# q and k of the first attention block: transposed by a trip through HBM and VectorE in place of TensorE

## The chip, the cores and the metric

The kernel runs on one core of one Trainium2 chip. The metric is device time in microseconds (us) of one execution of the whole layer, lower is better; the kernel before is given as the median of three runs. Engines are named as the profile names them: PE is TensorE (PEld its weight loads), DVE is VectorE, ACT is ScalarE, POOL is GpSimd and SP is SyncE, which here only issues transfers.

## The reference

One decoder layer on 256 tokens of width 2048, in float32. What the change touches is block A, a dilated sliding-window attention with 8 heads of 128; block B, a latent attention with 8 heads, the output projection and the MLP follow.

```python
h = _rmsnorm(x, norm_attn_pre)
proj = h @ w_in                        # columns: A.q | A.k | A.v | B.c_q | B.c_kv | B.k_rope
a_q = _rope(a_q.reshape(B, S, 8, 128), positions, 32)      # rotary on the first 32 of 128 channels
a_k = _rope(a_k.reshape(B, S, 8, 128), positions, 32)
...                                    # three windows: (128,1), (512,4), (2048,16), causal
s = einsum('...ihd,...jhd->...hij', q, k) * 128 ** -0.5    # per head: q times k transposed
p = exp(s - max(s)); o = (p / sum(p)) @ v                  # the three outputs merged by their sums
...
x = x + _rmsnorm(concat(A, B) @ w_out)
x = x + _rmsnorm(relu(rmsnorm(x) @ w_up) ** 2 @ w_down)
```

With 256 tokens the three windows fold into one softmax with a bias per query and key (a table that the host makes), so a head of block A is one score product, one softmax and one product with v.

## The kernel before

The tokens lie in two blocks of 128 (`b`), tokens on the partitions. Every big product is done in three passes over a value split in two (`hi` and `lo`: hi·hi, hi·lo, lo·hi), so each weight tile that comes from HBM into a `raw` buffer is rounded by ACT (`hi`, line 311) and subtracted by DVE (`lo`, line 312) before PE uses it. SP issues the weight loads (line 195). There are 5 `raw` buffers and 8 pairs of `hi` and `lo`, and a tile's split stands in the engines' queues 6 tiles ahead of the PE work that uses it.

The input projection of block A runs in two halves of four heads each: first `acc_qk` (q and k of heads 0 to 3 together), `acc_v`; then `acc_q`, `acc_k`, `acc_v` of heads 4 to 7; then the projections of block B (`acc_ckv`, `acc_cq`). ACT brings each result from PSUM to SBUF with the row's norm (`evac_a`, line 675), DVE applies the rotary table in four instructions (`rope`, lines 615 to 618).

The heads of a half (`heads_a`, line 651) are worked on while PE does the projections of what comes next. Per head: four PE transposes of a 128x128 piece of q or k into one PSUM bank (line 659, through the helper at line 305), one DVE copy of that bank to SBUF (`qkT_a`, line 661), the score product (`sc_a`, two matmuls, which show as four rows), the softmax on DVE and ACT, three more transposes (`pT_a`), and the product with v (`o_a`). Two chains of two heads each run at a distance of `D_PAIR`.

Each engine takes its instructions strictly in program order, and the program is written by a planner (`Flow`): every stretch of work is a generator that yields estimated waits, the planner keeps a clock that PE work moves on (0.109 us for a transpose, 0.216 us for a 512 column matmul), and between the matmuls of a projection it lets those generators write their next instructions whose due time has come. So a number in a `yield` decides between which matmuls an attention instruction stands on PE, and between which splits it stands on ACT and DVE.

In block A the host hands the tokens over in an order in which, inside a block of 128, token 32·(p mod 4) + p div 4 stands in row p. The MLP of the kernel uses this already: it writes 128x512 pieces of its middle result to HBM in another order (line 965), reads them back (line 978) and has DVE transpose the 32x32 blocks (line 980).

Of the kernel before, what the change touches and what calls it, by code (L numbers as in the profile page):

```python
# [26 lines left out]
P = 128  # L27
# [8 lines left out]
RA = 32  # L36
# [51 lines left out]
DA = (3.0, 0.5, 3.0, 3.0, 4.0, 3.0, 0.5)  # L88
DB = (2.5, 0.5, 2.0, 3.0, 3.0, 2.0)
D_PAIR, D_KR = 3.5, 10.0  # L90
D_X0, D_X, D_SS, D_TAB = 8.0, 3.0, 3.0, (14.0, 20.0)
D_NORM, D_HT, D_SECOND = 4.5, 1.5, 4.0

# [175 lines left out]
def layer(nc, tc, io):  # L269
# [23 lines left out]
    def tp_bank(name):  # L293
        return next_bank(4, 2, name)
# [214 lines left out]

    mix = pool("mix", "right")  # L510
    pa = pool("pa", "right")
    mixT = [mix.tile([P, HA + HB, S], F32R, name=f"mixT_{w}") for w in ("hi", "lo")]
    mix.tile([P, 64], F32, name="mix_pad")
    xT = [pa.tile([P, KD, S], F32R, name=f"xT_{w}") for w in ("hi", "lo")]
# [67 lines left out]
    def tables():  # L582

        yield D_TAB[0]
        nc.scalar.dma_start(out=pos_i, in_=io["pos"])
        nc.scalar.dma_start(out=cst, in_=io["consts"])
        yield D_TAB[1]
        pos_f = con.tile([P, NB], F32, name="pos_f")
        nc.vector.tensor_copy(pos_f, pos_i)
        ang = pa.tile([P, 2, NB, 96], F32, tag="qkT", bufs=2, name="ang")  # L590
        kk_ = pa.tile([P, 2, NB, 96], F32, tag="qkT", bufs=2, name="kk_")
        for w in range(2):
            for b in range(NB):
                nc.vector.tensor_scalar_mul(ang[:, w, b, :], freq[:, w * 96:(w + 1) * 96], pos_f[:, b:b + 1])
            nc.vector.tensor_scalar(kk_[:, w], ang[:, w], 1.0 / (2 * np.pi), 0.25 * w, op0=OP.mult, op1=OP.add)
        yield 1.0
        nc.vector.tensor_scalar(kk_, kk_, MAGIC, -MAGIC, op0=OP.add, op1=OP.add)
        for c in (C1, C2, C3):
            nc.vector.scalar_tensor_tensor(out=ang, in0=kk_, scalar=-c, in1=ang, op0=OP.mult, op1=OP.add)
        yield 1.0  # L600
        nc.vector.tensor_scalar_add(ang[:, 1], ang[:, 1], float(np.pi / 2))
        nc.vector.tensor_scalar(ang, ang, PI_LO, -PI_LO, op0=OP.min, op1=OP.max)
        yield 4.0
        nc.scalar.activation(trig, ang, AF.Sin)
# [43 lines left out]
        split(mixT[0][:, head, :], mixT[1][:, head, :], o[:, :S])  # L648


    def heads_a(qkv, half, hs, after):
        while any(c in flow.chains for c in after):
            yield 0.5
        for h in hs:
            nm = f"a{half}{h}"
            tp = tp_bank(f"qkT_{nm}")
            for i, w in enumerate("qk"):
                for b in range(NB):
                    transpose(tp[:, (2 * i + b) * P:(2 * i + b + 1) * P], qkv[w][:, b, h * 128:(h + 1) * 128])
            qkT = pa.tile([P, 512], F32, tag="qkT", bufs=2, name=f"qkT_{nm}")  # L660
            nc.vector.tensor_copy(qkT, tp)
            yield DA[0]
            sc = at_bank(f"sc_{nm}")
            mm(sc[:, 0:128], qkT[:, 0:128], qkT[:, 256:384], True, True, MM)
            mm(sc[:, 128:384], qkT[:, 128:256], qkT[:, 256:512], True, True, 2 * MM)
            yield DA[1]
            yield from softmax_pv(pa, DA, sc, bias_a, SCALE_A,
                                  [qkv["v"][:, b, h * 128:(h + 1) * 128] for b in range(NB)], half * 4 + h, nm)
            yield DA[6]

    def evac_a(t, accs, nm, half):
        while pre in flow.chains:
            yield 0.5
        for b in range(NB):
            nc.scalar.activation(t[:, b, :], accs[b][0], AF.Copy, scale=rstd0[0][:, b:b + 1])
        yield 1.0
        while tab in flow.chains:
            yield 0.5
        if nm != "v":
            tv = t.rearrange("p b (h d) -> p b h d", d=128)[:, :, :, :RA]  # L680
            rope(pa, tv, tv, RA // 2, 4, 0, f"{nm}{half}")

    pre = flow.start(prelude())
    tab = flow.start(tables())
# [1 line left out]
    for half in range(2):  # L686
        qkv = {}
        for nms in (("qk", "v") if not half else "qkv"):
            accs = [acc for _, _, acc in proj(xT, [ch_a[half, nms]], f"{nms}{half}",
                                              bank_of=at_bank if (half, nms) == (0, "v") else None)]  # L690
            for i, nm in enumerate(nms):
                t = pa.tile([P, NB, 512], F32, tag=nm, name=f"{nm}_{half}")
                qkv[nm] = t
                evacs.append(flow.start(evac_a(t, [[acc[i]] for acc in accs], nm, half)))
            flow.pump()
        flow.finish(*heads)
        heads = [flow.start(heads_a(qkv, half, hs, evacs), 2.0 + d) for hs, d in (((0, 1), 0.0), ((2, 3), D_PAIR))]


    lat = pool("lat", "left")  # L700
    ckv = lat.tile([P, NB, KVR + RB], F32, name="ckv")
    cq = lat.tile([P, NB, QR], F32, name="cq")
# [23 lines left out]
    for _, b, acc in proj(xT, [ch_ckv], "ckv"):  # L726
        for i in range(2):
            nc.scalar.activation(ckv[:, b, i * 288:(i + 1) * 288], acc[i][:, :288], AF.Copy, scale=rstd0[0][:, b:b + 1])
    kv_chain = flow.start(latent(ckv, 0, "kv", lat), 2.0)
    for _, b, acc in proj(xT, [ch_cq], "cq"):  # L730
        nc.scalar.activation(cq[:, b, :], acc[0], AF.Copy, scale=rstd0[0][:, b:b + 1])
    flow.finish(kv_chain, *heads)
# [658 lines left out]
```

## Time and profile before

| what | value |
|---|---|
| three runs | median 1036.33 us, 1035.93 to 1036.93 |
| the profiled execution | 1035.85 us |
| its span, first to last instruction | 1034.1 us |
| granted TensorE clock, mean | 0.997 |
| busy: PE, DVE, ACT, POOL | 1022.4, 834.4, 634.6, 63.5 us |
| instructions: PE, DVE, ACT, POOL | 4718, 1125, 850, 100 |
| moved by DMA | 253.44 MB, mean 245 GB/s |

The span is shorter than the profiled execution by 1.75 us, which lie outside the first and the last instruction. Matmuls are pipelined: the duration of one in the profile is longer than the time by which it puts off the next. The chain of waits gives the time that each piece of work held the end of the program back; that is the view in which PE work has a price.

### The profile page before, as it was taken

What the parts mean: (1) busy time and instruction counts of PE and PEld (TensorE: products, weight loads), DVE (VectorE), ACT (ScalarE), POOL (GpSimd) and SP (SyncE); (2) the same over time, 40 slices, a digit from 0 to 9 for tenths busy, and PEclk for the clock granted to TensorE, in tenths of its full rate; (3) what the DMA queues carried; (4) which work ended last, traced back from release to release, by engine and by line L of the source; (5) the groups of instructions that cost most, each with busy time, mean ns of one, the idle gap of its engine ahead of it and who ended that gap; (6) DMA issues with size and microseconds to landing.
All of it is one profiled execution on the core that took longest, in us unless ns stands there. A gap on an engine that the chain in (4) does not pass through costs nothing.

```text
span 1034.1 us, 13262 instructions
## 1 busy us (share of the span) xinstructions
PE 1022.4 (99%) x4718; PEld 851.3 (82%) x4718; DVE 834.4 (81%) x1125; ACT 634.6 (61%) x850; POOL 63.5 (6%) x100
## 2 busy tenths in 40 slices
PE   9999999999999999999999999999999999999996
PEld 6888889889888878888888888888888888888885
DVE  6675536577547669999999999898999999899795
ACT  6585536566446467666775767666666665767571
POOL 0000000000001010000100100000101000211100
PEclk9999999999999999999999999999999999999998
DMA  8975447554438478877989887589989867888962
GB/s 288 361 237 166 138 136 223 155 163 144 144 122 263 142 276 284 272 239 258 285 258 302 269 262 258 191 275 335 354 267 366 299 240 258 302 314 303 329 240 82
DMA packets 105298, 253.44 MB, mean 245 GB/s; under 512 B 8720, under 2 KB 29712, under 8 KB 104848
## 3 DMA queue, kind: packets, MB, share of 16 engines
q1 hardware_dynamic: 65744, 175.14, 50.8%
q0 software_dynamic: 16112, 57.68, 16.8%
q10 hardware_dynamic: 23376, 19.78, 6.1%
q8 instruction: 37, 0.61, 0.2%
q14 instruction: 29, 0.24, 0.1%
HBM read 224.78 MB, written 27.79 MB: 244 GB/s over the span
## 4 chain that ended last, share of the span: by engine, by line
PE 96%; DVE 1%; DMA 1%; issue 1%; ACT 0%; POOL 0%; DVEq 0%; POOLq 0%; SPq 0%; ACTq 0%
PE acc_u L301 26%; PE y L301 25%; PE acc_o L301 8%; PE md L301 6%; PE m L301 6%; PE acc_v L301 4%; PE acc_qk L301 4%; PE acc_ckv L301 2%; PE acc_ukv L301 2%; PE acc_q L301 2%; PE acc_cq L301 2%; PE acc_k L301 2%; PE acc_uq L301 2%; PE sc_b L301 1%; DMA raw<-in_w_in 1%
## 5 line engine op out<-in xcount | busy, mean ns | idle before, releaser
L312 DVE TENSOR_TENSOR lo<-raw,hi 128x1024 fp32r<-128x1024 f32 (+3 forms) x207 | 234.1, 1149 | 83.9 <-ACT hi L311 82.5
L311 ACT ACTIVATE hi<-raw 128x1024 fp32r<-128x1024 f32 (+3 forms) x207 | 203.4, 996 | 70.9 <-DMA raw<-in_w_in 16.8
L301 PE MATMUL acc_u<-hi,hT_lo 128*128 128x512 f32 x386 | 150.3, 389 | 0.4 <-DVE hT_lo L312 0.4
L301 PE MATMUL acc_u<-hi,hT_hi 128*128 128x512 f32 x386 | 150.7, 390 | 0.0
L301 PE MATMUL acc_u<-lo,hT_hi 128*128 128x512 f32 x386 | 150.2, 389 | 0.0
L301 PE MATMUL y<-hi,uhi 128*128 128x512 f32 x358 | 139.3, 389 | 0.0
L301 PE MATMUL y<-lo,uhi 128*128 128x512 f32 x358 | 139.3, 389 | 0.0
L301 PE MATMUL y<-hi,ulo 128*128 128x512 f32 x358 | 139.3, 389 | 0.0
L315 ACT ACTIVATE hi<-raw,gcol 128x1024 fp32r<-128x1024 f32 x86 | 97.0, 1148 | 33.1 <-PE acc_u L301 18.2
L316 DVE SCALAR_TENSOR_TENSOR lo<-raw,gcol,hi 128x1024 fp32r<-128x1024 f32 x86 | 106.7, 1273 | 9.4 <-ACT hi L315 9.3
L301 PEld LDWEIGHTS acc_u<-hi,hT_lo 128*128 128x128 f32 x386 | 72.5, 188 | 15.9 <-DVE hT_lo L312 0.8
L301 PEld LDWEIGHTS acc_u<-lo,hT_hi 128*128 128x128 f32 x386 | 72.5, 188 | 14.9
L301 PEld LDWEIGHTS acc_u<-hi,hT_hi 128*128 128x128 f32 x386 | 72.5, 188 | 14.7
L301 PEld LDWEIGHTS y<-hi,uhi 128*128 128x128 f32 x358 | 67.2, 188 | 14.1
L301 PEld LDWEIGHTS y<-lo,uhi 128*128 128x128 f32 x358 | 67.2, 188 | 13.9
L301 PEld LDWEIGHTS y<-hi,ulo 128*128 128x128 f32 x358 | 67.2, 188 | 13.9
L312 DVE TENSOR_TENSOR lo<-st_down,hi 128x1024 fp32r<-128x1024 f32 x46 | 55.0, 1219 | 0.6 <-ACT hi L311 0.6
L301 PE MATMUL acc_o<-hi,mixT_hi 128*128 128x512 f32 x128 | 51.8, 405 | 0.0
L311 ACT ACTIVATE hi<-u 128x1024 fp32r<-128x1024 f32 (+1 forms) x33 | 32.2, 979 | 29.7 <-PE acc_u L301 11.7
L301 PE MATMUL acc_o<-hi,mixT_lo 128*128 128x512 f32 x128 | 50.2, 392 | 0.0
L301 PE MATMUL acc_o<-lo,mixT_hi 128*128 128x512 f32 x128 | 50.0, 390 | 0.0
L311 ACT ACTIVATE hi<-st_down 128x1024 fp32r<-128x1024 f32 x46 | 47.8, 1049 | 3.5 <-DVE st_down L371 2.1
(338 smaller groups left out, 2018.9 us busy)
## 6 DMA issues: line engine op xcount, KB each, us to landing
raw<-in_w_up SPq DMA_DIRECT2D x86, 512.0 KB, 4.8
raw<-in_w_down SPq DMA_DIRECT2D x82, 512.0 KB, 6.1
raw<-in_w_in SPq DMA_DIRECT2D x55, 512.0 KB, 5.1
ab<-in_w_up POOLq DMA_DIRECT2D x17, 1024.0 KB, 7.4
raw<-in_w_out SPq DMA_DIRECT2D x32, 512.0 KB, 4.4
ab_down<-in_w_down POOLq DMA_DIRECT2D x11, 1024.0 KB, 8.9
ulo<-ukeep POOLq DMA_DIRECT2D x20, 512.0 KB, 6.4
rkeep<-r ACTq DMA_DIRECT2D x28, 256.0 KB, 3.4
```

The lines of the kernel that those rows point to most:

```text
L301: nc.tensor.matmul(out, a, b, start=start, stop=stop)
L311: nc.scalar.activation(hi, src, AF.Copy)
L312: nc.vector.tensor_tensor(out=lo, in0=src, in1=hi.bitcast(F32), op=OP.subtract)
L315: nc.scalar.activation(hi, src, AF.Copy, scale=g)
L316: nc.vector.scalar_tensor_tensor(out=lo, in0=src, scalar=g, in1=hi.bitcast(F32), op0=OP.mult, op1=OP.subtract)
```

## The change

The PE transposes of q and k and the DVE copy behind them are gone. Instead, after the rotary step, each of q and k of a half makes a trip: POOL issues two stores (one per token block, 256 KB each) to a scratch tensor in HBM in an order that puts every 32x32 block's channels next to each other, then two loads that bring it back, and DVE transposes the 32x32 blocks of the returned tile into the place from which the score product reads. To make room for the trip the tiles of q and k have three slots of 512 columns in place of two (ACT writes slots 1 and 2, DVE writes slots 0 and 1), and those of the first half lie in a pool of their own (`early`) that is given up before block B's latents are placed. ACT writes q and k in another column order (channels of the four heads interleaved in groups of 32), so its read from PSUM is strided.

New waits in the planner: 2.0, 5.0 and 13.0 (first half) or 9.0 (second) between rotary step, stores, loads and DVE transposes, and a delay of 2.5 before the heads start. The first half's heads so stand later in the program; before v of the second half is brought from PSUM they are now finished.

```diff
+D_LOADED, D_LATENT = (13.0, 9.0), 3.5
...
+    early = pool("early", "left")
...
-    def heads_a(qkv, half, hs, after):
+    def heads_a(qkv, half, hs, after, delay):
         while any(c in flow.chains for c in after):
             yield 0.5
+        yield delay
         for h in hs:
             nm = f"a{half}{h}"
-            tp = tp_bank(f"qkT_{nm}")
-            for i, w in enumerate("qk"):
-                for b in range(NB):
-                    transpose(tp[:, (2 * i + b) * P:(2 * i + b + 1) * P], qkv[w][:, b, h * 128:(h + 1) * 128])
-            qkT = pa.tile([P, 512], F32, tag="qkT", bufs=2, name=f"qkT_{nm}")
-            nc.vector.tensor_copy(qkT, tp)
-            yield DA[0]
+            qT, kT = [qkv[w][:, :2, h * P:(h + 1) * P] for w in "qk"]
             sc = at_bank(f"sc_{nm}")
-            mm(sc[:, 0:128], qkT[:, 0:128], qkT[:, 256:384], True, True, MM)
-            mm(sc[:, 128:384], qkT[:, 128:256], qkT[:, 256:512], True, True, 2 * MM)
+            mm(sc[:, 0:128], qT[:, 0], kT[:, 0], True, True, MM)
+            mm(sc[:, 128:384], qT[:, 1], kT, True, True, 2 * MM)
...
         for b in range(NB):
-            nc.scalar.activation(t[:, b, :], accs[b][0], AF.Copy, scale=rstd0[0][:, b:b + 1])
+            out, a = t[:, b + (nm != "v"), :], accs[b][0]
+            if nm != "v":
+                out, a = [v.rearrange(f"p ({o}) -> p a h c", a=4, h=4) for v, o in ((out, "a h c"), (a, "h a c"))]
+            nc.scalar.activation(out, a, AF.Copy, scale=rstd0[0][:, b:b + 1])
...
-        if nm != "v":
-            tv = t.rearrange("p b (h d) -> p b h d", d=128)[:, :, :, :RA]
-            rope(pa, tv, tv, RA // 2, 4, 0, f"{nm}{half}")
+        if nm == "v":
+            return
+        tv = t[:, 1:, :128].rearrange("p b (h d) -> p b h d", d=RA)
+        rope(pa, tv, tv, RA // 2, 4, 0, f"{nm}{half}")
+        keeps = [dram.tile([P, 512], F32, name=f"keep{nm}{half}{b}") for b in range(NB)]
+        yield 2.0
+        for b in range(NB):
+            nc.gpsimd.dma_start(out=keeps[b].rearrange("(a t) (q c) -> (t q) a c", a=4, q=4),
+                                in_=t[:, b + 1, :].rearrange("m (a c) -> m a c", a=4))
+        yield 5.0
+        for b in range(NB):
+            nc.gpsimd.dma_start(out=t[:, b + 1, :], in_=keeps[b])
+        yield D_LOADED[half]
+        for b in range(NB):
+            nc.vector.transpose(t[:, b, :].rearrange("p (h t q) -> p h q t", h=4, q=4),
+                                t[:, b + 1, :].rearrange("p (q h c) -> p h q c", q=4, h=4))
+            yield 1.0
...
+                if half and nm == "v":
+                    flow.finish(*heads)
+                if not half and nm != "v":
+                    t = early.tile([P, NB + 1, 512], F32, name=f"{nm}_{half}")
+                else:
+                    t = pa.tile([P, NB + (nm != "v"), 512], F32, tag=nm, name=f"{nm}_{half}")
...
-        heads = [flow.start(heads_a(qkv, half, hs, evacs), 2.0 + d) for hs, d in (((0, 1), 0.0), ((2, 3), D_PAIR))]
+        heads = [flow.start(heads_a(qkv, half, hs, evacs, d), 2.0) for hs, d in (((0, 1), 2.5), ((2, 3), 2.5 + D_PAIR))]
+    early.release()
...
-    kv_chain = flow.start(latent(ckv, 0, "kv", lat), 2.0)
+    kv_chain = flow.start(latent(ckv, 0, "kv", lat), D_LATENT)
```

(The scratch tiles of the rotary table, `ang` and `kk_`, took the buffers of `qkT` before and take those of the softmax, `s`, now. Line numbers of the changed kernel are higher by 1 to 20.)

How the change moves instructions is shown at three places. On PE, before, at the end of the second weight tile of `acc_q` (the second half's q): the second head's transposes (`qkT_a`) and the first head's scores.

```order
L301 MATMUL acc_q_0_1_0_706<-hi_593,xT_hi 128x512
L301 MATMUL acc_q_0_1_0_706<-lo_594,xT_hi 128x512
L301 MATMUL acc_q_0_1_0_706<-hi_593,xT_lo 128x512
L305 MATMUL qkT_a_750<-ident,q_524 128x128 x2
L305 MATMUL qkT_a_750<-ident,k_525 128x128 x2
L301 MATMUL sc_a_757<-qkT_a_730 128x128
L301 MATMUL sc_a_757<-qkT_a_730 128x256
L301 MATMUL acc_q_0_0_0_705<-hi_632,xT_hi 128x512
```

The same work now: the first score product of the block, at the end of the sixth weight tile of `acc_q`.

```order
L302 MATMUL acc_q_0_1_0_721<-hi_701,xT_hi 128x512
L302 MATMUL acc_q_0_1_0_721<-lo_702,xT_hi 128x512
L302 MATMUL acc_q_0_1_0_721<-hi_701,xT_lo 128x512
L302 MATMUL sc_a_834<-k_528,q_527 128x128
L302 MATMUL sc_a_834<-k_528,q_527 128x256
L302 MATMUL acc_q_0_0_0_720<-hi_724,xT_hi 128x512
```

The first scores moved from 24 to 72 matmuls behind the start of `acc_q`, and no transposes stand before them.

On DVE, before, after the splits that follow the first half's rotary steps (`lo_710` is the seventh weight tile of `acc_q`):

```order
L312 TENSOR_TENSOR lo_710<-raw_707,hi_709 128x1024 [waits DMAHW1_49,PE_49,Activation_49]
L661 COPY qkT_a_730<-qkT_a_725 128x512 [waits PE_49]
L312 TENSOR_TENSOR lo_735<-raw_732,hi_734 128x1024 [waits DMAHW2_49,Activation_49]
L661 COPY qkT_a_755<-qkT_a_750 128x512 [waits PE_49]
L626 ISA s_a_760,st_a_761<-sc_a_757,cst 128x128 [waits PE_49]
```

Now (`lo_725` is that same tile, `lo_761`, `lo_779`, `lo_799` and `lo_819` are the first four of `acc_k`; DMASW are semaphores of POOL's transfers):

```order
L313 TENSOR_TENSOR lo_725<-raw_722,hi_724 128x1024 [waits DMAHW1_49,PE_49,Activation_49]
L313 TENSOR_TENSOR lo_743<-raw_740,hi_742 128x1024 [waits DMAHW2_49,PE_49,Activation_49]
L313 TENSOR_TENSOR lo_761<-raw_758,hi_760 128x1024 [waits DMAHW3_49,Activation_49]
L313 TENSOR_TENSOR lo_779<-raw_776,hi_778 128x1024 [waits DMAHW4_49,Activation_49]
L693 STREAM_TRANSPOSE q_527<-q_527 128x4x4x32 [waits DMASW4_49]
L693 STREAM_TRANSPOSE k_528<-k_528 128x4x4x32 [waits DMASW6_49,DVE_49]
L313 TENSOR_TENSOR lo_799<-raw_796,hi_798 128x1024 [waits DMAHW5_49,Activation_49]
L693 STREAM_TRANSPOSE q_527<-q_527 128x4x4x32 [waits DMASW5_49,DMASW0_49,DVE_49]
L693 STREAM_TRANSPOSE k_528<-k_528 128x4x4x32 [waits DMASW7_49,DMASW2_49,DVE_49]
L313 TENSOR_TENSOR lo_819<-raw_816,hi_818 128x1024 [waits DMAHW6_49,Activation_49]
```

The copies that waited for PE are gone; four transposes that wait for POOL's loads stand among the splits instead.

POOL's queue, before, around the same stage:

```order
L506 TENSOR_TENSOR rstd_pre<-t_pre,neg_half 128x2 [waits DVE_49]
L506 TENSOR_TENSOR rstd_kv<-t_kv,neg_half 128x2 [waits DVE_49]
L506 TENSOR_TENSOR rstd_q<-t_q,neg_half 128x2 [waits DVE_49]
L743 MEMSET krT 128x512 [waits PE_49,Activation_49]
L506 TENSOR_TENSOR rstd_pw<-t_pw,neg_half 128x2 [waits DVE_49]
```

Now, for the first half (the same eight follow for the second half, with q's ahead of k's, before `rstd_kv`):

```order
L507 TENSOR_TENSOR rstd_pre<-t_pre,neg_half 128x2 [waits DVE_49]
L686 DMA keepq_624<-q_527 128x4x128 [waits DVE_49,Activation_49]
L686 DMA keepq_625<-q_527 128x4x128 [waits Activation_49]
L686 DMA keepk_632<-k_528 128x4x128 [waits DVE_49,Activation_49]
L686 DMA keepk_633<-k_528 128x4x128 [waits Activation_49]
L690 DMA q_527<-keepq_624 128x512 [waits DMASW0_49]
L690 DMA q_527<-keepq_625 128x512 [waits DMASW1_49]
L690 DMA k_528<-keepk_632 128x512 [waits DMASW2_49]
L690 DMA k_528<-keepk_633 128x512 [waits DMASW3_49]
```

Sixteen transfers of 256 KB stand in POOL's queue between `rstd_pre` and `rstd_kv`, and each load waits for its store to have landed.

More of the change, by code (lines that the diff above doesn't have):

```diff
@@ L589, in tables @@
         nc.vector.tensor_copy(pos_f, pos_i)
-        ang = pa.tile([P, 2, NB, 96], F32, tag="qkT", bufs=2, name="ang")
-        kk_ = pa.tile([P, 2, NB, 96], F32, tag="qkT", bufs=2, name="kk_")
+        ang = pa.tile([P, 2, NB, 96], F32, tag="s", bufs=2, name="ang")
+        kk_ = pa.tile([P, 2, NB, 96], F32, tag="s", bufs=2, name="kk_")
         for w in range(2):
```

1 line of the change is left out of this document (removed).

## The prediction

> **What bounds the kernel now.** I read the page's busy times first, then what PE waits for, then the chain of waits through the stage that is changed. The busy line, the chain by engine's first row, and all waits of PE:
>
> ```profile
> PE 1022.4 (99%) x4718; PEld 851.3 (82%) x4718; DVE 834.4 (81%) x1125; ACT 634.6 (61%) x850; POOL 63.5 (6%) x100
> PE acc_qk L301 <- ACT hi L311: 1.3, 3, 0.6
> PE warm L526 <- DVE zero L523: 1.2, 1, 1.2
> PE acc_u L301 <- DVE hT_lo L312: 0.4, 1, 0.4
> PE qrt L305 <- DVE qT L777: 0.2, 1, 0.2
> ```
>
> PE never rests for long: its waits sum to 3.1 us, and none lies in the changed stage. So a microsecond of PE work taken out there is a microsecond off the end, as long as nothing that PE needs comes later than it does now. The stage runs from the first `acc_v` (50.95) to the end of `acc_cq` (203.5). The chain through it, by line, and its first pieces (start us, us, what):
>
> ```profile
> by line: PE acc_v L301 28.5%; PE acc_ckv L301 16.8%; PE acc_q L301 14.4%; PE acc_cq L301 14.4%; PE acc_k L301 14.4%; PE sc_a L301 3.4%; PE o_a L301 3.4%; PE qkT_a L305 2.3%; PE pT_a L305 1.7%; PE ckvt L305 0.6%; PE acc_qk L301 0.1%
> 50.95 21.76 PE acc_v L301 x96
> 72.72 2.73 PE acc_q L301 x12
> 75.44 0.44 PE qkT_a L305 x4
> 75.88 2.76 PE acc_q L301 x12
> 78.64 0.44 PE qkT_a L305 x4
> 79.08 0.66 PE sc_a L301 x4
> ```
>
> The whole chain there is PE. A projection matmul costs 21.76 / 96 = 0.2267 us, a group of four transposes of q and k 0.44 us.
>
> **What the change removes.** From PE, 8 groups of four transposes: 8 x 0.44 = 3.52 us, which the 2.3% of the 152.55 us of the stage confirms (3.51). It also removes interruptions: 12 matmuls behind a group take 2.76 us where 12 undisturbed ones take 2.73 us, so an interruption costs about 0.03 us more. By PE's order there were 25 groups of attention or latent work between projection matmuls in this stage and there are 17 now: 8 x 0.03 = 0.24 us, between bounds of 0 and 0.5. Expected from PE: 3.5 + 0.2 = **3.7 us**.
>
> The rows of the transposes on PE and the copy behind them (ns min/median/max):
>
> ```profile
> L305 PE MATMUL qkT_a<-ident,q x16: 270/272/273, 75.3 to 175.9; 128*128 128x128 f32 x16
> L305 PE MATMUL qkT_a<-ident,k x16: 272/273/273, 75.5 to 176.1; 128*128 128x128 f32 x16
> L661 DVE COPY qkT_a<-qkT_a x8: 678/692/692, 75.9 to 176.5; 128x512 f32<-128x512 f32 x8
> L980 DVE STREAM_TRANSPOSE uT<-c x16: 665/702/707, 467.9 to 600.1; 128x512 f32<-128x512 f32 x16
> ```
>
> Priced by the duration of one, 32 x 0.272 would be 8.7 us; the chain shows that one puts off the next by 0.44 / 4 = 0.11 us, and that is the price I take. The Trainium skill ("TensorE: Matmul & The Clock Gate", Part 4: PE-mode transpose) gives about 390 ns for one bf16 transpose alone and about 275 ns inside a kernel, and its page "VectorE: DVE Perf Modes" (Rules for kernel authors) advises TensorE for 128x128 transposes, against this change. By 390 ns the gain would be 12.5 us, an estimate from that page; the trace has the 272 ns as a duration but 110 ns on the path, and the trace decides.
>
> On DVE 8 copies of 0.69 us go and 8 block transposes of 128x512 come; the MLP's at line 980 take 0.70 us. That is a draw; if the new strided write doubled it, 8 x 0.7 = 5.6 us would be added to a DVE that is busy 39 of the 74 us from 72.7 to 146.8 (17.58 + 21.50 in the rows below). ACT's eight reads of q and k are strided now; at most double their 0.69 us would be 5.5 us, on an ACT that is busy 34 of these 74 us. Both lie beside PE and I cost them at nothing; the splits of weights that share these queues are the cover, and their lead over PE is worked out below.
>
> ```profile
> 72.70:102.00 29.30, 29.30 (x148) 24.64 (x147) 17.58 (x37) 15.74 (x25) 0.00 (x0) 1.00 0.67 208
> 102.00:146.80 44.80, 44.80 (x204) 37.08 (x204) 21.50 (x37) 18.57 (x31) 0.00 (x0) 1.00 0.45 132
> ```
>
> (Columns: stretch; busy PE, PEld, DVE, ACT, POOL; clock; DMA share; GB/s.)
>
> **What it adds: the trip.** The score product now needs rotary step, store, load and block transpose. The first half has the least time. Its rotary steps and a weight split on DVE, POOL's state before, how long a transfer holds POOL, and times to landing (issue line: KB each, median us):
>
> ```profile
> 67.48 0.42 DVE L618 TENSOR_TENSOR q<-rp_q,rp_q 128x256 f32<-128x256 f32 x1
> 68.87 0.42 DVE L618 TENSOR_TENSOR k<-rp_k,rp_k 128x256 f32<-128x256 f32 x1
> 74.42 1.22 DVE L312 TENSOR_TENSOR lo<-raw,hi 128x1024 fp32r<-128x1024 f32 x1 [0.58 <-ACT hi L311]
> 64.57 0.71 POOL L506 TENSOR_TENSOR rstd_pre<-t_pre,neg_half 128x2 f32<-128x2 f32 x1 [63.23 <-DVE t_pre L505]
> 492.07 0.97 POOL L1006 DMA_DIRECT2D ukeep<-uT  x1
> L1036 POOL DMA_DIRECT2D ulo<-ukeep x20: 528/536/561, 715.0 to 984.7; - x20
> rkeep<-r ACTq DMA_DIRECT2D x28, 256.0 KB, 3.4
> c<-rkeep ACTq DMA_DIRECT2D x28, 256.0 KB, 4.9
> x<-in_x SPq DMA_DIRECT2D x8, 256.0 KB, 7.0
> ulo<-ukeep POOLq DMA_DIRECT2D x20, 512.0 KB, 6.4
> DMA to landing us min/median/max: 2.3/4.7/13.2
> ```
>
> The last row is for all transfers to and from `rkeep`, which have the same two shapes as the new ones but go by ACT's queue. A store here has four pieces per partition; I take 1.0 us of POOL for it (0.97 is the longest 256 KB row) and 0.54 us for a load. q is ready at 67.90, k at 69.29, POOL is free since 65.28: the stores are issued at 67.9, 68.9, 69.9 and 70.9. Per leg the bounds are 2.3 and 13.2 us; I take 7.0, the row of the 256 KB loads of x, since they ran in a stage as full of weight loads as this one. The third store (first block of k) so lands at 76.9 and its load at 83.9, the fourth pair 1 us later. In DVE's order the split of the second `acc_k` tile stands ahead of the transposes; it waits until PE has freed its buffer, eight tiles back, the second `acc_q` tile: 72.72 + 24 x 0.2267 = 78.2. With ACT's and DVE's part of the split DVE stands at the transposes at about 80.5 and waits for the trip some 3 us. The transposes of the first blocks end at 83.9 + 0.7 = 84.6, a split of 1.22 us follows, and the second blocks' two end at 87.2.
>
> PE asks at 72.72 + 72 x 0.2267 = 89.0, since the first scores stand behind 72 matmuls of `acc_q` that nothing interrupts any more. **Slack: 1.8 us**. With the legs of 3.4 and 4.9 DVE's own work sets it: 80.5 + 4 x 0.7 + 1.2 = 84.5, slack 4.5 us. What queues behind the waiting transposes on DVE is the split of the third `acc_k` tile. PE needs it after 96 matmuls of `acc_q`, two scores (0.66 each) and 24 of `acc_k`: 72.72 + 120 x 0.2267 + 1.3 = 101.2. A DVE that gets to it at 85 is 16 us early, so this wait costs nothing. POOL has nothing else to do here: the next in its queue is `rstd_kv`, of block B's latents, behind `acc_ckv`.
>
> The second half has more room. Rows of the chain for it and of the DMA's load (page, 40 slices; weights' landing):
>
> ```profile
> 125.02 21.76 PE acc_v L301 x96
> 149.61 3.19 PE acc_ckv L301 x24
> GB/s 288 361 237 166 138 136 223 155 163 144 144 122 263 142 276 284 272 239 258 285 258 302 269 262 258 191 275 335 354 267 366 299 240 258 302 314 303 329 240 82
> raw<-in_w_in SPq DMA_DIRECT2D x55, 512.0 KB, 5.1
> ```
>
> q's trip starts after `acc_q` (about 96), k's after `acc_k`, at 125.0 less four removed groups, about 123; rotary step, two stores, two legs of 7 and the transposes end near 142. Its first scores stand behind `acc_v` (21.76), one `o_a` (0.65) and 42 matmuls of `acc_ckv` (42 x 3.19 / 24 = 5.6): near 151. Slack 9 us.
>
> The 4 MB of trips come on top of the 208 and 132 GB/s above: 2 MB in the 29.3 us of the first row are 72 GB/s more, 280 in all, while the slices show up to 366. The weights' landing of 5.1 us may grow by a few microseconds against that lead of 16.
>
> The heads' later places cost PE nothing in themselves: the same scores, `pT_a` and `o_a` are done, the last `o_a` with 51 matmuls of `acc_cq` to go (33 before), so block B, which waits for all heads, isn't held.
>
> **The sum.** Against its own execution: 1035.85 - 3.7 = 1032.1 us. The median of the runs shown lies 0.48 us higher (1036.33), and so the forecast is **1032.6 us**. A change below 0.2% (2.07 us) could not be told from none here.
>
> **The rivals.** Two of them rest on the MLP's stretches, in the columns given above, and on what DVE's splits wait for:
>
> ```profile
> 450.00:692.00 242.00, 242.00 (x1069) 200.45 (x1068) 225.06 (x250) 165.22 (x190) 16.47 (x21) 1.00 0.82 262
> 692.00:1015.00 323.00, 323.00 (x1427) 267.54 (x1426) 297.53 (x341) 205.16 (x232) 32.21 (x52) 1.00 0.84 294
> DVE lo L312 <- ACT hi L311: 100.9, 94, 5.3
> ```
>
> *The trip is late for the first half* (ends slower). PE stands at the first score product until the last load has landed and been transposed, and nothing behind it on PE may pass. The last transpose ends at 69.9 + two legs + three transposes of 0.7 (q's first has gone ahead) + a split of 1.2, that is at 73.2 + legs; against 89.0 the stall begins when the legs together exceed 15.8 us, eats the gain at 19.5 and is slower by more than 0.2% from 21.6. At the longest landing for both (26.4) it is 10.6 us: 1043 us. For it: 13.2 occurs, and the stores meet the busiest weight loading of the block. Against: medians of 3.4 to 7.0 sum to 14 at most. Chance 0.07 for slower, and 0.09 for a stall of 1.7 to 5.7 us that leaves the time within 0.2%, near 1035.5.
>
> *POOL issues the trip slowly* (slower, 0.02 of the 0.07). If the DVE work beside it stretched each of POOL's eight issues to 3 us, the load of k's first block would be the seventh, issued by 67.9 + 21 = 88.9; with 6.5 us to its landing and 3.3 us of DVE work the last transpose would end at 98.7, a stall of 9.7 us, 1042 us. Against it: the 0.97 us issue stands in a stage where DVE is 93% busy (225.06 of 242 us). The Trainium skill ("SBUF — State Buffer", the box on the "DVE blocks DMA" trap in "SBUF: two separate sides") states such a rule: a DMA issued from GpSimd waits for its descriptors while VectorE holds the shared port, about 3.1 us in place of 0.62 beside one kind of copy. By that rule this rival is the outcome; no POOL issue in this trace is that long, so the trace speaks against it.
>
> *The gain is taken back in the MLP* (no change). DVE is nearly full there (225.06 of 242 and 297.53 of 323 us). If DVE set the pace there, PE's earlier arrival would be waited away: 1036.3 us. Against: PE waits 0.4 us in all of the MLP, and DVE itself waits for ACT's `hi`, which waits for buffers that PE frees; a PE that comes 3.7 us earlier moves them along. Chance 0.04.
>
> *Transposes cost other than the chain shows.* If the pieces that follow closed up, less than 3.5 us would come off, down to perhaps 2.0: 1034.3 us. Within the forecast's own range mostly; below 2.07 us 0.02.
>
> **How the numbers follow.** The forecast, faster by 3.7 with a stall below 1.6 us, has 0.78; its own range is 1031.8 to 1034.2. No change has 0.09 + 0.04 + 0.02 = 0.15, slower 0.07. The range for 8 in 10 leaves out the slower side and half of no change: **1031.4 to 1035.2**, the lower end 0.3 us below for interruptions at their upper bound and 0.9 us for the scatter of a median, since the three runs of before lie 1.0 us apart.
>
> **What would show it.** Right: no `qkT_a` group on PE; the stage to the end of `acc_cq` shorter by 3.5 to 4 us; no wait of PE at `sc_a`; the last block transposes of the first half ended before 89; DVE waiting there for POOL's loads, a few microseconds. Wrong: a PE wait at the first `sc_a` of either half, or POOL's issues far above 1 us, or new waits of PE for `hi` or `lo` after 66, or the stage shorter but the span not.

## The result and the profile after

| | before | changed |
|---|---|---|
| median, us | 1036.15 (16 runs, 1035.00 to 1037.67) | 1033.78 (16 runs, 1032.50 to 1035.70) |
| ratio, 95% interval | | 0.9978 [0.9971, 0.9985] |
| span of the profiled execution | 1034.1 | 1032.2 |
| first `acc_v` to the end of `acc_cq` | 152.56 | 150.57 |
| first `y` to the end | 341.1 | 342.2 |

The change gains 2.4 us, some two thirds of the 3.7 that the prediction summed up. In the stage that is changed it gains 2.0. The page of the changed kernel shows the removed work (32 matmul records fewer on PE, 4.2 MB more on the DMA):

```profile
PE 1020.1 (99%) x4686; PEld 849.0 (82%) x4686; DVE 836.8 (81%) x1125; ACT 633.4 (61%) x850; POOL 74.3 (7%) x116
DMA packets 106579, 257.65 MB, mean 250 GB/s; under 512 B 8976, under 2 KB 29968, under 8 KB 106128
```

The waits of PE in the changed kernel (us in total, times, longest us; those left out stood in the kernel before too). The first row is new and lies in the changed stage:

```profile
PE pT_a L306 <- DVE st_a L637: 1.2, 1, 1.2
...
PE y L302 <- DVE lo L313: 0.4, 1, 0.4
PE y L302 <- DVE ulo L313: 0.2, 1, 0.2
...
```

The chain of waits through the stage (start us, us, what), at its two places of interest. At the first scores it stays on PE, but `sc_a` takes 0.92 us where the next one takes 0.66. In the second half it leaves PE for ten microseconds, of which PE itself rests only the last 1.2:

```profile
49.92 21.76 PE acc_v L302 x96
71.69 16.32 PE acc_q L302 x72
88.00 0.92 PE sc_a L302 x4
...
92.37 0.66 PE sc_a L302 x4
...
170.56 0.67 PE o_a L302 x4
...
178.42 0.72 ACT junk_kv L731 x2
179.14 0.37 ACT mixT_hi L316
179.54 0.49 DVE mixT_lo L317
180.06 0.48 ACT mixT_hi L316
180.56 0.48 DVE mixT_lo L317
181.19 0.52 PE pT_a L306 x3
```

The trip of the first half went as follows on POOL and on DVE (timelines: start us, us, instruction, in brackets the idle time before it and what ended it):

```profile
67.79 1.70 POOL L686 DMA_DIRECT2D keepq<-q  x2 [3.23 <-DVE q L620]
69.48 1.50 POOL L686 DMA_DIRECT2D keepk<-k  x2
75.97 0.54 POOL L690 DMA_DIRECT2D k<-keepk  x1 [0.33 <-DMA keepk<-k]
```

```profile
82.17 1.08 DVE L693 STREAM_TRANSPOSE q<-q 128x512 f32<-128x512 f32 x1
83.10 1.06 DVE L693 STREAM_TRANSPOSE k<-k 128x512 f32<-128x512 f32 x1
85.00 1.22 DVE L313 TENSOR_TENSOR lo<-raw,hi 128x1024 fp32r<-128x1024 f32 x1 [0.84 <-ACT hi L312]
86.14 1.10 DVE L693 STREAM_TRANSPOSE q<-q 128x512 f32<-128x512 f32 x1
87.08 1.09 DVE L693 STREAM_TRANSPOSE k<-k 128x512 f32<-128x512 f32 x1
```

POOL issues two stores in 1.70 and two in 1.50 us, a load in 0.54. DVE waits for no load: its own splits bring it to the transposes at 82.2. The last transpose ends at 87.08 + 1.09 = 88.17, and PE asks at 88.00.

So three places could hold the missing time, and they are the theories of the experiments: the new wait at `pT_a` (the order of heads and latents), the trip itself (late transposes, its DVE work, its load on the queues), and the MLP, whose last stretch is 1.1 us longer in this pair of profiles.

### The profile page after: what moved, and what is told of

Its sections match the earlier page's. It is cut to its first block, busy times and chain, and to the rows that moved or that the text cites. A ratio compares the mean times of both kernels' runs of the same rounds, so it can differ in the third digit from the quotient of the medians.

```text
span 1032.2 us, 13250 instructions
## 1 busy us (share of the span) xinstructions
PE 1020.1 (99%) x4686; PEld 849.0 (82%) x4686; DVE 836.8 (81%) x1125; ACT 633.4 (61%) x850; POOL 74.3 (7%) x116
## 3 DMA queue, kind: packets, MB, share of 16 engines
q1 hardware_dynamic: 65744, 175.14, 50.6%
## 4 chain that ended last, share of the span: by engine, by line
PE 85%; DVE 7%; DMA 3%; ACT 3%; issue 2%; ACTq 0%; POOL 0%; DVEq 0%; POOLq 0%; SPq 0%
PE acc_u L302 23%; PE y L302 19%; PE acc_o L302 8%; PE md L302 5%; PE m L302 5%; PE acc_qk L302 4%; PE acc_v L302 4%; DVE lo L313 3%; PE acc_ckv L302 2%; PE acc_ukv L302 2%; PE acc_k L302 2%; PE acc_q L302 2%; PE acc_cq L302 2%; PE acc_uq L302 2%; DMA rkeep<-uT 1%
## 5 line engine op out<-in xcount | busy, mean ns | idle before, releaser
L302 PE MATMUL acc_u<-hi,hT_hi 128*128 128x512 f32 x386 | 150.7, 390 | 0.0
```

What stands on the lines that cost most here:

```text
L302: nc.tensor.matmul(out, a, b, start=start, stop=stop)
```

## The experiments

### The changed kernel again, and the latents later

The first run is the changed kernel a second time. The second changes one number, so that block B's latents (`ckvt` on PE, `junk_kv` and `mixT` on ACT and DVE) start later.

> The changed kernel, unchanged, a second time: what does its profile repeat? In the first profile the stage from the first acc_v to the end of acc_cq was 1.99 us shorter than before instead of the forecast 3.7, with a PE wait of 1.2 us at pT_a (for DVE's softmax scale) and a first sc_a of 0.92 us, and the last stretch (first y to the end) was 1.1 us longer. Theory (the missing time lies in the stage, at pT_a): the wait at pT_a returns at 1.0 to 1.4 us, stage 150.3 to 150.9, time 1033 to 1034.5. Rival (the MLP gives it back): the last stretch is again over 1 us longer than before's. Rival (chance): the pT_a wait is gone or moved, and the stretch of y comes out like before's.

```diff
-D_LOADED, D_LATENT = (13.0, 9.0), 3.5
+D_LOADED, D_LATENT = (13.0, 9.0), 5.5
```

> One number of the changed kernel altered: block B's latents (kv chain) start 5.5 in place of 3.5 planner microseconds after their projection, so that on ACT and DVE their work stands behind the softmax scale of the second half's last-but-one head, and on PE that head's pT_a ahead of ckvt. Theory (the head's softmax was held by the latents' work queued ahead of it): the PE wait of 1.2 us at pT_a goes, no new wait above 0.3 us comes, the stage is 149.2 to 149.7 instead of 150.57, time about 1.0 to 1.2 us below the changed kernel, 1032.7. Rival (the trip is what costs, by late transposes or DMA load): the wait moves to another place of the same size, time as the changed kernel, 1033.8. Rival (the MLP gives it back): the stage gets shorter, the time doesn't.

Again: 1032.88 us, ratio 0.997 [0.9959, 0.9981], the wait at `pT_a` again 1.2 us, the stage 150.7; the first scores have a wait of their own here, 0.2 us. Latents at 5.5: 1032.99 us, 0.997 [0.996, 0.9981], the stage 150.3 and not the expected 149.2 to 149.7; no gain. The wait moved to the next head's `pT_a` and has another name. The first row is a wait of PE, the others the chain there:

```profile
PE pT_a L306 <- DVE mixT_lo L317: 1.0, 1, 1.0
```

```profile
180.13 0.34 PE pT_a L306 x3
...
181.69 0.72 ACT junk_kv L731 x2
...
183.84 0.50 DVE mixT_lo L317
184.33 0.14 issue
184.47 0.52 PE pT_a L306 x3
```

My theory, that the softmax scale of the head (`st_a`, the name in the wait's row) was late behind the latents' work, falls. By the letter the rival on the trip came true (the wait moved, the time stayed); the run without the trip, below, decides against it. In the changed kernel the head that waits had its scaled scores long before. In DVE's timeline there, 177.13 is the reciprocal of the head that waits, and 180.97 that of the next head:

```profile
177.13 0.16 DVE L637 RECIPROCAL st_a<-st_a 128x2 f32<-128x2 f32 x1
177.33 0.55 DVE L639 TENSOR_SCALAR s_a<-s_a,st_a 128x128 f32<-128x128 f32 x2
...
180.56 0.48 DVE L317 SCALAR_TENSOR_TENSOR mixT_lo<-ckvt,gcol,mixT_hi 128x256 fp32r<-128x256 f32 x1 [0.54 <-ACT mixT_hi L316]
180.97 0.15 DVE L637 RECIPROCAL st_a<-st_a 128x2 f32<-128x2 f32 x1
```

The scores were ready at 177.9; PE went on at 181.19, 0.15 us after the second `mixT_lo` had ended (181.04). In the run with latents at 5.5 it went on 0.13 us after the second `mixT_lo` too (184.34), and the scores had been ready since 179.4. `pT_a` reads only the scores and writes only its bank, so what both wait for is the **PSUM bank**, the piece of memory that PE writes its result into. PE's transposes share two banks in turn (`tp_bank`, two banks): `ckvt`, `ckvt`, `pT_a` makes `pT_a` reuse the bank of the first `ckvt`, and that one is empty only when ACT, behind the two squares `junk_kv`, and DVE have each read it twice. The releaser that the profile names is the instruction that ended last on DVE before PE went on. In the kernel before, 27 matmuls (6.17 us) stood between the last `ckvt` and the next `pT_a`, and the bank was free by then (the chain there):

```profile
181.89 0.43 PE ckvt L305 x4
182.33 6.17 PE acc_cq L301 x27
188.50 0.33 PE pT_a L305 x3
```

Now nothing stands there. The last `ckvt` in PE's timeline of the changed kernel; the next row there is the `pT_a` of 181.19:

```profile
179.37 0.60 PE L306 MATMUL ckvt<-ident,ckv 128*128 128x128 f32 x4
```

### Scores later too, and the changed kernel without the trip

The next run keeps the latents at 5.5 and starts the first half's heads 1.4 later.

```diff
-        heads = [flow.start(heads_a(qkv, half, hs, evacs, d), 2.0) for hs, d in (((0, 1), 2.5), ((2, 3), 2.5 + D_PAIR))]
+        heads = [flow.start(heads_a(qkv, half, hs, evacs, d if half else d + 1.4), 2.0) for hs, d in (((0, 1), 2.5), ((2, 3), 2.5 + D_PAIR))]
```

> As the run with latents at 5.5, and the first half's heads start 1.4 planner microseconds later too: the first sc_a stands behind 81 matmuls of acc_q instead of 72, 2 us later on PE. Theory: the wait at pT_a goes (1.2 us) and the first sc_a falls from 0.92 to 0.66 us, since the last block transpose (ends at 88.2) is then early by 1.8 us; together 1.2 + 0.26 = 1.46 us, stage 149.1, time about 1032.3. Rival (the heads moved later collide with other work, as the second half's did): a new PE wait at pT_a or o_a of the first half, time 1033 or more. Rival (the MLP gives it back): stage 149.1 and the time as the changed kernel, 1033.8.

Without the trip, which leaves out the stores, the loads and the block transposes:

```diff
-            qT, kT = [qkv[w][:, :2, h * P:(h + 1) * P] for w in "qk"]
+            qT, kT = [qkv[w][:, 1:, h * P:(h + 1) * P] for w in "qk"]
...
-        for b in range(NB):
-            nc.gpsimd.dma_start(out=keeps[b].rearrange("(a t) (q c) -> (t q) a c", a=4, q=4),
-                                in_=t[:, b + 1, :].rearrange("m (a c) -> m a c", a=4))
...
-            nc.gpsimd.dma_start(out=t[:, b + 1, :], in_=keeps[b])
...
-            nc.vector.transpose(t[:, b, :].rearrange("p (h t q) -> p h q t", h=4, q=4),
-                                t[:, b + 1, :].rearrange("p (q h c) -> p h q c", q=4, h=4))
```

> The changed kernel without the trip: the two stores, two loads and two block transposes of each of q and k are left out, and the scores read the tiles as ACT and the rotary step left them, so that the scores are of other numbers; the order on PE is the changed kernel's. Theory (the trip itself costs PE only the 0.26 us at the first sc_a; the rest is the place of the heads against the latents): the first sc_a falls to 0.66, the wait at pT_a stays at 0.9 to 1.2 us, time 0.2 to 0.5 us below the changed kernel, 1033.4. Rival (the trip is what takes back the gain, by its DVE work of 8 x 1.07 = 8.6 us, its 4 MB on the DMA queues or POOL's issues): the wait at pT_a goes as well, the stage falls to 149.1, time 1032.3 or less.

Scores later: 1032.96 us, 0.9969 [0.9958, 0.9979]; the first `sc_a` takes 0.66 us as expected, but the stage is 150.08 and not 149.1: the wait of 1.0 us at `pT_a` stays as in the run with latents at 5.5. Without the trip: 1033.97 us, 0.9977 [0.9967, 0.9986]. Its stage is 150.24 us. Its wait at `pT_a` and its first scores:

```profile
PE pT_a L306 <- DVE st_a L637: 1.2, 1, 1.2
```

```profile
88.02 0.66 PE sc_a L302 x4
```

With all stores, loads and block transposes gone the 1.2 us are still there. The trip's 4.2 MB, POOL's issues and DVE's extra work are not what makes them; in this stage the trip costs PE some 0.3 us, 0.26 of it at the first scores. The time was not forecast rightly: it was to be 0.2 to 0.5 us below the changed kernel and lies 1.1 above the one measured beside it (1032.88). In its one profile the way from the end of `acc_cq` to the first `y` is 0.7 us longer than in that kernel's (490.3 us, 489.6 there); why, no run shows.

### The latents behind all heads

```diff
-D_LOADED, D_LATENT = (13.0, 9.0), 3.5
+D_LOADED, D_LATENT = (13.0, 9.0), 10.0
```

(and the first half's heads 1.4 later, as above.)

> Block B's latents start 10 planner microseconds after their projection (3.5 in the changed kernel, 5.5 in the last two runs), so that on ACT and on PE they stand behind the softmax and the transposes (pT_a) of all heads of the second half; the first half's heads start 1.4 later as in the run 'both'. With latents at 5.5 the wait of 1.2 us at pT_a only moved to the next head's pT_a (1.0 us, for mixT_lo), whose PSUM bank is freed by latent work that stands on ACT behind the squares (junk_kv). Theory (the order of latents and heads on ACT makes the wait): no PE wait above 0.2 us between the first acc_v and the end of acc_cq; that stage 149.0 to 149.3 (before 152.56, changed kernel 150.57). Time, if nothing is given back later: 1.0 below the run 'both', -3.7 to -3.9 against the kernel before. Rival (the MLP gives back: between 945 and 980 the DMA is at 100% and PE waits for lo there): stage as said, the time not more than 0.3 us below 'both' (-2.9 against before) and a longer wait at y, 1.0 us or more. Rival (some other engine work takes the place): the wait moves a third time.

> The run with latents at 10 and the first half's heads 1.4 later, a second time, since its median (1031.39) lies 1.6 us below the run 'both' where the stage is only 1.3 us shorter, and its fall against the kernel before (-5.4) exceeds the stage's -3.8. Theory (PE's stage gives -3.8, the rest was scatter of the start and of y's stretch): stage 148.7 to 148.9, no PE wait in it, time 3.6 to 4.6 below the kernel before. Rival (something beyond the stage got shorter too): time 5 or more below.

1031.39 us, ratio 0.9947 [0.9934, 0.9959], and the second time 1032.11 us, 0.9958 [0.9945, 0.997]. Of the PE waits only those outside the stage are left, and the chain stays on PE from end to end:

```profile
...
PE acc_qk L302 <- ACT hi L312: 0.9, 2, 0.7
PE acc_u L302 <- DVE hT_lo L313: 0.4, 1, 0.4
...
```

```profile
by line: PE acc_v L302 29.3%; PE acc_ckv L302 17.2%; PE acc_k L302 14.7%; PE acc_cq L302 14.7%; PE acc_q L302 14.6%; PE sc_a L302 3.5%; PE o_a L302 3.5%; PE pT_a L306 1.8%; PE ckvt L306 0.6%; PE acc_qk L302 0.2%; PE acc_ukv L302 0.2%
```

The stage is 148.78 us, the second time 148.77: 3.78 less than before, where the prediction had 3.52 + 0.24 = 3.76 for the removed transposes and interruptions. The expected stage was 149.0 to 149.3. This version is faster than the kernel before by 5.5 and 4.4 us in the two runs, with intervals from 3.1 to 6.8 us, and its stage is 1.8 us shorter than the changed kernel's. Both gains are above the stage's 3.8. The last stretch is 341.0 and 342.5 us in its two profiles, and the first `acc_v` starts at 50.3 and 50.6; neither shows where 0.6 us or more beyond the stage would be. That stays open; the second interval holds the stage's 3.8, the first ends at 4.3.

### Does PE's gain reach the end?

The MLP as the place where the gain is given back is asked by a dose, that is by leaving out a known amount of PE work ahead of it, and by a second profile of the kernel before.

```diff
                         for p, (x, w) in enumerate(passes):
+                            if name.startswith("o") and k % 4 == 0 and (x, w) == (0, 1):
+                                flow.spend(MM)
+                                continue
                             mm(accs[c][b][j][:, :m], tok(aT[x], k, b), wt[w][:, kk, o:o + m],
```

> A dose: the changed kernel with 32 of the 384 acc_o matmuls (the pass lo times hi for every fourth k) left out, so that PE reaches the MLP 32 x 0.2267 = 7.25 us earlier; the output loses precision, everything else is the changed kernel's. Theory (PE is the bound to the end): the time falls by 6.5 to 7.3 us against the changed kernel, about 1026, and y's waits stay below 1 us in sum. Rival (the DMA-full stretch at 945 to 980 sets the end once PE comes earlier): the time falls by 5 us or less, and PE waits at y for lo by 2 us or more.

> The kernel before, unchanged, for a second profile of it: which stretch scatters between executions? Theory (the stretch from the first y to the end scatters with the DMA, the stage of block A doesn't): stage from the first acc_v to the end of acc_cq 152.4 to 152.7 as in the first profile (152.56), from the first y to the end 341.2 to 343. Rival (the scatter lies in the start): the first acc_v differs by over 0.5 us from 50.95.

The dose: 1027.08 us, 0.9907 [0.9893, 0.992], that is 9.7 us below the kernel before measured beside it. The changed kernel was 2.4 and 2.95 us below in its two measurements, so 7.25 us of PE work are worth 6.7 to 7.3, give or take 1.5 or more by the intervals. From the end of `acc_cq` to the first `y` the dose takes 482.9 us, 6.7 less than the 489.4 to 489.6 that both profiles of the kernel before, both of the changed kernel and both with the latents behind all heads have there: what is gained in the stage reaches `y` whole, and of the dose two new waits ahead of `y` (0.4 us more at `qrt`, 0.2 at `acc_o`) keep some 0.6. The waits at `y` sum to 1.2 us, over the 1 that was expected, but the second measurement of the changed kernel has 1.5 there without any dose. The second profile of the kernel before has this kind of wait too (0.4 us), and its stage is 152.56 us to the hundredth. From the first `y` to the end it has 342.3 us. The kernel before so lies at 341.1 and 342.3 there, the versions of the changed kernel at 341.0 to 343.2. The 1.1 us of the first pair lie within this scatter, and the MLP takes nothing back that stands out of it; a few tenths could hide in it. The start scatters also: the first `acc_v` lies between 49.7 and 51.5 in all these profiles.

### The price of a transpose

```diff
-                    transpose(tp[:, (2 * i + b) * P:(2 * i + b + 1) * P], qkv[w][:, b, h * 128:(h + 1) * 128])
+                    for _ in range(2):
+                        nc.tensor.transpose(tp[:, (2 * i + b) * P:(2 * i + b + 1) * P], qkv[w][:, b, h * 128:(h + 1) * 128], ident)
+                    flow.spend(TR)
```

> The kernel before with each PE transpose of q and k done twice into the same place (32 more of them, nothing else moved). By the price of the chain (0.11 us each, 0.44 for four): a group of eight holds PE 0.88 us, time +3.5 us. By the duration of one (0.272): +8.7. By the Trainium skill's figure for one alone (390 ns, page 'TensorE: Matmul & The Clock Gate', Part 4) +12.5. Rival (the pieces close up): below +2.

1040.82 us, ratio 1.0035 [1.0024, 1.0045], that is +3.6 us by the ratio and +4.1 by the medians; the stage went from 152.56 to 156.05, +3.49. Divided by 32 that is 0.109 us for one. Its chain:

```profile
75.96 0.87 PE qkT_a L660 x8
76.83 2.77 PE acc_q L301 x12
```

### Scores with no slack behind the trip, and the strided write

```diff
-D_LOADED, D_LATENT = (13.0, 9.0), 3.5
+D_LOADED, D_LATENT = (6.0, 9.0), 3.5
```

> The changed kernel with the planner's wait between the loads and the block transposes of the first half cut from 13 to 6, so that PE asks for the first scores after 39 matmuls of acc_q instead of 72, 7.5 us earlier (80.3 by the changed kernel's profile). Theory (the trip alone then sets the start of the heads): the load of k's first block, issued at 75.1, lands 5.6 us later at 80.7; a block transpose (1.08), a split (1.22) and two more block transposes follow, to 85.2: PE waits 4.9 us at the first sc_a, the time rises by 4.5 to 5 us over the changed kernel, to about 1038. Rival (landing is what scatters, up to 13 us): a wait of 8 us or more. Rival (the wait is made good, since the heads end earlier and the pT_a wait of 1.2 us of the second half goes): time +3.5 or less.

> The run with the first scores 33 matmuls earlier, unchanged, for a second profile: ten executions of it lie in two groups, five at 1036.9 to 1037.4 (the profiled one among them, with 2.1 us of waiting at sc_a) and five at 1039.6 to 1041.3. Theory (with no slack the time takes on the scatter of the trip's transfers): in an execution of the second group the wait at sc_a is 4 to 6 us and the loads of k land later by as much. Rival (another stretch makes the second group): the wait at sc_a is 2 us as before and y's stretch or another is 3 us longer. If the profiled execution falls in the first group again, this stays open.

Ten executions gave 1036.9 to 1037.4 five times and 1039.6 to 1041.3 five times (median 1038.50, ratio 1.0026 [1.0015, 1.0038]). The median fits the "about 1038" that was expected, but by chance: no execution lies between the two groups. The first profile is of an execution of 1036.85, the second of one of 1040.81. The first scores in the timeline of PE, with the idle time before them in brackets, first and second profile (the last row is from the chain there):

```profile
82.41 0.46 PE L302 MATMUL sc_a<-k,q 128*128 128x128 f32 x2 [0.78 <-DVE k L693]
84.17 0.70 PE L302 MATMUL sc_a<-k,q 128*128 128x256 f32 x2 [1.30 <-DVE k L693]
```

```profile
83.40 0.77 PE L302 MATMUL sc_a<-k,q 128*128 128x128 f32 x2 [2.78 <-DVE k L693]
85.15 1.22 PE L302 MATMUL sc_a<-k,q 128*128 128x256 f32 x2 [0.99 <-DVE k L693]
86.37 4.97 PE acc_q L302 x15
```

The trip does set the start of the heads here, as the theory says, and its waits, 2.1 and 3.8 us in sum, are shorter than my 4.9 us: no split stood between the last transposes, and PE itself came later than in the profile from which I took its 80.3. The rival that the landing scatters widely falls, and with it the theory for the second profile, since k's loads landed within 5.8 to 6.1 us in both. What differs is the start: in the second execution the projections began 1.0 us earlier and the stores 0.6 us later. But the second execution's stage is 4.1 us longer than the first's (156.9 and 152.8 us), of which the wait explains 1.7. The rest is in the scores, whose two rows above are 0.83 us longer, and in the last row: 15 matmuls of `acc_q` took 4.97 us instead of 3.42. The stretches there (columns as in the prediction; the clock is the third number from the end) tell why, first profile, then second:

```profile
80.00:84.00 4.00, 2.09 (x10) 1.31 (x8) 2.82 (x4) 2.28 (x3) 0.00 (x0) 1.00 1.04 386
84.00:86.00 2.00, 1.83 (x8) 1.57 (x9) 2.00 (x3) 1.12 (x1) 0.00 (x0) 1.00 0.32 113
```

```profile
80.00:84.00 4.00, 1.22 (x5) 0.69 (x3) 1.83 (x2) 1.45 (x2) 0.00 (x0) 0.84 1.04 385
84.00:86.00 2.00, 1.01 (x4) 0.76 (x3) 2.00 (x3) 1.95 (x2) 0.00 (x0) 0.50 0.61 225
86.00:88.00 2.00, 2.00 (x6) 1.52 (x6) 1.97 (x8) 0.00 (x0) 0.00 (x0) 0.50 0.36 55
88.00:90.00 2.00, 2.00 (x7) 1.57 (x6) 1.18 (x2) 0.99 (x4) 0.00 (x0) 0.62 0.95 296
```

In the second execution the granted clock of PE was at half for some 6.8 us (0.32 of the first 4 us, all of the next 4, 0.76 of the last 2): from about 82.7, inside the rest of 2.78 us, to 89.5. In the first, with rests of 0.78 and 1.30 us, it did not fall.

The strided write was measured by itself:

```diff
-            nc.vector.transpose(t[:, b, :].rearrange("p (h t q) -> p h q t", h=4, q=4),
+            nc.vector.transpose(t[:, b, :].rearrange("p (h q t) -> p h q t", h=4, q=4),
```

> The changed kernel with the block transposes writing their 32 columns next to each other instead of at a stride of 16 bytes; the tokens then stand in another order for the scores, so that these are of other pairs of tokens. Theory (the strided write makes a block transpose 1.07 us where the MLP's takes 0.70): 0.69 to 0.71 us each, the first sc_a at 0.66 us instead of 0.92. Rival (the strided read, or float32 with the other shape, makes it): 1.0 us or more.

q's transposes by shape (busy us, mean ns), first the changed kernel, then this one; k's are alike, 1077 and 688 ns:

```profile
L693 DVE STREAM_TRANSPOSE q<-q 128x512 f32<-128x512 f32 x4 | 4.3, 1080 | 0.0
```

```profile
L693 DVE STREAM_TRANSPOSE q<-q 128x512 f32<-128x512 f32 x4 | 2.8, 704 | 0.0
```

The strided write alone makes 0.70 us into 1.08. The last transpose then ended at 86.1, and the first `sc_a` took 0.66 us. The time of its one execution, 1034.67 us, says nothing beside a scatter of 3 us.

## Why the prediction was right, and where it was wrong

**The direction and the bound held.** PE is the bound, and what is taken from it comes off the end: the dose of 7.25 us showed it, against the rival that the MLP takes the gain back.

**The price of the removed work held.** 8 groups at 0.44 us and 8 interruptions at 0.03 us were to give 3.76 us; with the waits gone the stage is shorter by 3.78. The doubled transposes give 0.109 us each. By the durations (0.272 us) the gain would have been 8.7, by the Trainium skill's 390 ns ("TensorE: Matmul & The Clock Gate", Part 4) 12.5, an estimate from that page; neither is what a transpose in a dense stream costs PE.

**The step that failed is "the heads' later places cost PE nothing in themselves".** I looked at when heads must be finished (the last `o_a`, 51 matmuls ahead) and not at what stands next to them. In the second half the third head's scores even stand earlier than before (after 156 matmuls of `acc_ckv`, 180 before), because the step of the PE transposes ahead of them is gone, while the latents start later (3.5 for 2.0). So `pT_a` came to stand directly behind two `ckvt` that hold both banks. From the start of `acc_ckv` to the end of `acc_cq` the changed kernel takes 56.36 us, with the latents behind all heads 54.86: the wait of 1.2 us and the refilling of PE behind it cost 1.50.

**The block transposes were mis-sized**: 0.70 us was the row of a dense write, 1.08 is the strided one; the bound of twice 0.70 that I kept did hold it. DVE came to them at 82.2 and not at 80.5, and their last ended at 88.17 in place of 87.2. The other half of the lost slack is PE's: in this execution its projections began 1.03 us earlier (first `acc_v` 49.92, before 50.95), and the trip, whose stores I had at 67.9 and which began at 67.8, did not. So the slack of 1.8 us became a lack of 0.17; my sum had no term for a start of PE that scatters against the trip. From the first `acc_v` to `acc_ckv` the changed kernel takes 94.21 us, with the scores 9 matmuls later 93.92: 0.29. Together 1.50 + 0.29 = 1.79 us of the 3.78, which leaves the 1.99 that the stage shows.

**The trip's legs** were shorter than I took them (7.0; the sixteen of the first profile 2.9 to 6.8 us, k's two loads of the first half 5.7 and 6.2), POOL's stores cheaper (0.75 to 0.94 us against 1.0). ACT's strided reads of q and k, for which I allowed up to double, take 0.68 to 0.70 us as before. "DVE waits some 3 us for the loads" was wrong: it waits for none. The rival of slow POOL issues falls: while the four stores were issued DVE was busy for 3.87 of 3.90 us (the third busy time of this row, columns as above).

```profile
67.70:71.60 3.90, 3.90 (x19) 3.24 (x18) 3.87 (x7) 3.68 (x5) 3.75 (x5) 1.00 0.56 132
```

The 3.1 us that the Trainium skill ("SBUF — State Buffer", "A bandwidth-pool intuition that's wrong (but worth ruling out)") gives for a DMA from this queue beside one kind of copy are not seen in these issues beside this DVE work, splits and rotary steps.

**The forecast** of 1032.6 us was 1.2 us low, inside its range of 1031.4 to 1035.2. That it held owes more to the width of the range than to the sum. Of the signs named for being right, the stage shorter by 3.5 to 4 us and DVE's wait for the loads did not come; of those for being wrong, a wait at the first `sc_a` came in the second measurement, 0.2 us. The stage misses 1.8 us of the 3.76 and the medians only 1.3 of the 3.7; I take the difference for scatter of the start and the MLP, which no run settles.

## What to carry to other kernels

A work item that is moved in a hand-made order is to be costed by its new neighbours on every shared resource, the PSUM banks in rotation too: ask which tile had the bank before, and when its last reader gets to it. The releaser that a profile names for a wait is the last event on that engine, not always the thing waited for; if the operand was ready long before, look for the buffer. And a transfer that feeds PE wants a slack of some microseconds, because a rest of PE of two to three microseconds can cost it its clock as well.

## What the runs showed of the hardware

- A rest of PE of 2.78 us brought some 6.8 us at a granted clock of 0.50 (15 matmuls in 4.97 us in place of 3.42), rests of 0.78 and 1.30 us none. That more than doubled the price of the wait; the two groups of executions, some 3 us apart, fit it, and so do their mean granted clocks (0.994 to 0.997 in the slower group, 0.996 to 0.998 in the faster), though only one execution of each was profiled. The Trainium skill ("TensorE: Matmul & The Clock Gate", Part 1) has the clock at half after an idle window of about 3.4 us; the fall to half agrees with the trace, but a recorded rest of 2.78 us was enough here.
- How a rest lies in time counts too. In the clock records of all 14 profiles the stretches at full clock are whole multiples of 3.413 us long (78.51 is 23 of them, 1020.59 is 299, 1024.00 is 300), so the clock changes on a fixed grid. It fell at the end of a grid interval in which PE's records leave 2.05 us or more idle (2.09 here; 2.05 behind the last matmul of the second run with the latents behind all heads), and it stayed up after intervals with 1.89 us idle (behind the last matmul of the run with the dense write) or less.
- A block transpose of 128x512 float32 on DVE takes 0.70 us with a dense write and 1.08 with columns written 16 bytes apart.
- POOL's issue of a 256 KB store in four pieces per partition takes 0.75 to 0.94 us, with DVE 99% busy beside it.
